# One GpSimd power in place of the Newton steps of the norms, two multiplications moved from GpSimd to VectorE, and the low part of the key copied over 128 partitions

## The chip, the cores and the metric

The kernel runs on one core of a Trainium2 chip. A core has TensorE (PE in the profile; its weight loads are listed apart as PEld), VectorE (DVE), ScalarE (ACT), GpSimd (POOL), and SyncE (SP), whose queue issues nearly all DMAs here. The metric is the device time of one execution in microseconds (us); less is better.

## The reference

The program is a two-layer encoder trunk on 512 tokens of width 1024. Each layer has a mixer (differential attention with 4 heads beside a bidirectional gated recurrence), a cross attention into 256 memory tokens and a squared-ReLU MLP, each behind an RMS norm. What the change touches:

```
y = x * rsqrt(mean(x*x) + 1e-6) * g                       # every norm
q, k = partial_rope(q), partial_rope(k)                   # t1*c - t2*s, t2*c + t1*s
s1, s2 = (q[..., 0] @ k1.T) / 8, (q[..., 1] @ k2.T) / 8   # two score maps of a head, 64 wide each
o = (softmax(s1) - lam * softmax(s2)) @ v
o = rms_norm(o, subln_g) * (1 - lam_init)                 # per head
u = x * i * sqrt(1 - a*a)                                 # i: a sigmoid gate, per channel and direction
```

All is computed in float32 accuracy: each operand of a product is split into a high and a low part, and a product is the sum of high x high, high x low and low x high.

## The kernel before, in words

**Layout.** Activations lie feature-major, 128 features by 512 tokens in a tile. A weight tile of 128x1024 is loaded (wraw), rounded by ScalarE to its high part (whi), and VectorE subtracts to get the low part (wlo). Tiles named b are 128x512 buffers (62 of them), s are columns of up to 8 numbers, mm and at are PSUM banks, pt holds transposed probabilities.

**Order of work.** Nothing is emitted where it is written. Every call is recorded with a key, which is the amount of TensorE work recorded before it (less a lead for loads and attention steps), and a list scheduler (Plan, from line 151; it emits at line 412) places the operations from a table of assumed costs (cost). Each engine then runs its instructions strictly in the order so found, so an operation that comes later than assumed holds up whatever stands behind it on its engine. All instructions therefore carry one line, 412; their tiles tell them apart.

**Layer.** First the value product and the norm of the input, then head 0's query and key. After that 16 attention steps (4 heads, 4 blocks of 128 queries), each with a piece of other work between its parts (fill): the query and key of the next heads (qk_head), the convolutions, gates and scans of the recurrence (lru_conv, lru_gates, lru_scan), the memory's keys and values. These stages lie at about 46 to 262 us in layer 0 and 785 to 1016 us in layer 1. Then come output projection, cross attention and MLP.

**Norms.** Norm.rstd (line 550) sums squares with TensorE against a column of ones, VectorE scales the sums (ms), rsqrt_small (line 495) computes ms to the power -1/2 by an integer guess and three Newton steps: ten VectorE instructions on at most 4 columns, each reading the one before. bcast (line 507) then spreads the columns with four TensorE transposes. There are 18 such roots: per layer three norms of x, one of the recurrence's output and four of the heads; one of the memory; and the final norm.

**Rotation and gates.** In qk_one (line 798) VectorE shuffles the product's partitions, multiplies it by the cosine table, GpSimd multiplies the shuffled copy by the sine table Sr, and VectorE adds: 16 times in all. In lru_gates (line 717) GpSimd multiplies the convolution's output by each input gate, also 16 times.

**Scores.** For one half j of a head, qk_head (line 814) stacks by DMA two 64-row parts of the query: m0 is high above low, m1 low above high. s0 and s1 hold the key's high part of half j twice, one copy over the other. So one product of 128 rows gives qh.kh + ql.kh. The rest, qh.kl, is a second product of 64 rows, taken from partitions 0 to 63 for j = 0 and 64 to 127 for j = 1:

```
PE.matmul(sc, mq, s_, start=True, stop=False)
PE.matmul(sc, m_[64 * j:64 * j + 64, qc * P:(qc + 1) * P],
          kl[64 * j:64 * j + 64, :], start=False, stop=True)
```

A step has two such pairs, a layer 32, the program 64.

Of the kernel before, what the change touches and what calls it, by code (L numbers as in the profile page):

```python
# [11 lines left out]
F32 = mybir.dt.float32  # L12
F32R = mybir.dt.float32r
I32 = mybir.dt.int32
AF = mybir.ActivationFunctionType
ALU = mybir.AluOpType
AX = mybir.AxisListType

P = 128
# [131 lines left out]
class Plan:  # L151
# [43 lines left out]
    def cost(self, eng, m, a, k):  # L195
        out = a[0] if a else k["out"]
        n = 1
        for d in out.shape[1:]:
            n *= d
        if eng == "pe":  # L200
            if m == "transpose":
                return 0.109
            f32 = a[1].root.dtype == F32
            if n < 64:
                return 0.224
            return n * 0.00176 if f32 else max(0.114, n * 0.000456)
        if m == "dma_start":
            return 0.06
        if eng == "act":
            t = 0.093 + n * 0.000833  # L210
            t += 0.093 * sum(isinstance(k.get(x), _View) for x in ("scale", "bias", "accum_out"))
            return t
        if eng == "dve":
            if m == "tensor_reduce":
                n = 512
            if m == "tensor_scalar_mul":
                return 0.066 + n * 0.0007
            ap = m == "scalar_tensor_tensor" and isinstance(a[2], _View)
            return 0.067 + n * 0.00105 + 0.06 * ap
        if eng == "pool":  # L220
            return 0.1 + n * (0.0022 if m != "memset" else 0.001)
        return 0.06
# [192 lines left out]
def trunk(tc, ctx, xT, memT, pos, W, par, outT):  # L415
# [10 lines left out]
    V, A, G, PE, SP = (plan.engine(e) for e in ("dve", "act", "pool", "pe", "sp"))  # L426

    def C(shape, dt, name):
        return plan.tile("c_" + name, shape, dt)

    def R():
        return plan.tile("b", [P, S], F32R)

    def T():
        return plan.tile("b", [P, S], F32)

    def SM(n):
        return plan.tile("s", [P, n], F32)

    def MM():  # L440
        return plan.tile("mm", [P, S], F32)

    def AT():
        return plan.tile("at", [P, S], F32)

    def b(v):
        return v.bitcast(F32)
# [24 lines left out]
    def weight(l, t):  # L472
        raw = pre.pop(t, None) if l == 0 else None
        first = raw is not None
        if raw is None:
            raw = raw_weight(l, t)
        hi = plan.tile("whi", [P, 1024], F32R)
        lo = plan.tile("wlo", [P, 1024], F32R)
        with plan.ahead(SPLIT_AHEAD):
            for cs in (slice(0, 512), slice(512, 1024)) if first else (slice(0, 1024),):  # L480
                split(hi[:, cs], lo[:, cs], raw[:, cs])
        return hi, lo

    def gemm_fm(l, t, xs, out, order=range(KD)):

        hi, lo = weight(l, t)
        for i, k in enumerate(order):
            xh, xl = xs[k]
            wh = hi[:, k * P:(k + 1) * P]
            with plan.group():  # L490
                PE.matmul(out, wh, xh, start=(i == 0), stop=False)
                PE.matmul(out, wh, xl, start=False, stop=False)
                PE.matmul(out, lo[:, k * P:(k + 1) * P], xh, start=False, stop=(i == KD - 1))

    def rsqrt_small(ms, n):

        y = SM(n)
        V.tensor_scalar(y.bitcast(I32), ms.bitcast(I32), -0.5, 1597463007.0,
                        op0=ALU.mult, op1=ALU.add)
        for _ in range(3):  # L500
            t = SM(n)
            V.tensor_tensor(t, y, y, op=ALU.mult)
            V.scalar_tensor_tensor(t, t, -0.5, ms, op0=ALU.mult, op1=ALU.mult)
            V.scalar_tensor_tensor(y, t, 1.5, y, op0=ALU.add, op1=ALU.mult)
        return y

    def bcast(col, ncol, out):
# [17 lines left out]
    def pc(l, name, i):  # L525
        o = l * NPL + PC[name] + i
        return prm[:, o:o + 1]
# [4 lines left out]
                    pattern=[[-1, P]], channel_multiplier=1)  # L532
    ones = C([P, P], F32, "ones")
    G.memset(ones, 1.0)

    class Norm:

# [179 lines left out]
    def lru_gates(l, pr, conv, neg, posi):  # L717

        gh, gl = weight(l, T_G + pr)
        gs = {}  # L720
        for c2 in range(2):
            c = 2 * pr + c2
            cc, ch, cl = conv[c]
            for d in range(2):
                for q in range(2):
                    pm = MM()
                    o = (4 * c2 + 2 * d + q) * P
                    with plan.group():
                        PE.matmul(pm, gh[:, o:o + P], ch, start=True, stop=False)
                        PE.matmul(pm, gh[:, o:o + P], cl, start=False, stop=False)  # L730
                        PE.matmul(pm, gl[:, o:o + P], ch, start=False, stop=True)
                    t = T()
                    A.activation(t, pm, AF.Sigmoid, bias=pc(l, "b_i" if q else "b_r", d * 4 + c))
                    if q:
                        G.tensor_tensor(t, cc, t, op=ALU.mult)
                    gs[c2, d, q] = t
        av = {}
        for c2 in range(2):
            for d in range(2):
                r = gs[c2, d, 0]  # L740
                col = l * 8 + d * 4 + 2 * pr + c2
                a, a2 = T(), T()
                A.activation(a, r, AF.Exp, scale=neg[:, col:col + 1])
                A.activation(r, r, AF.Tanh, scale=posi[:, col:col + 1])
                A.activation(a2, a, AF.Square)
                V.scalar_tensor_tensor(r, a2, 1.0, r, op0=ALU.add, op1=ALU.mult)
                av[c2, d] = a
        return gs, av
# [49 lines left out]
    def qk_one(l, t, xs, Cr, Sr, scale):  # L798
        pm = MM()
        gemm_fm(l, t, xs, pm)  # L800
        sh, q = T(), T()
        V.stream_shuffle(sh, pm, SHUF)
        V.tensor_tensor(q, pm, Cr, op=ALU.mult)
        G.tensor_tensor(sh, sh, Sr, op=ALU.mult)
        V.tensor_tensor(q, q, sh, op=ALU.add)
        hi, lo = R(), R()
        if scale is None:
            split(hi, lo, q)
        else:
            A.activation(hi, q, AF.Copy, scale=scale)  # L810
            V.scalar_tensor_tensor(lo, q, scale, b(hi), op0=ALU.mult, op1=ALU.subtract)
        return hi, lo

    def qk_head(l, h, xs, Cr, Sr):
        dm = SP.dma_start
        qh, ql = qk_one(l, T_FM + 2 * h, xs, Cr, Sr, 0.125)
        m0, m1 = R(), R()
        dm(out=b(m0[0:64, :]), in_=b(qh[0:64, :]))
        dm(out=b(m0[64:128, :]), in_=b(ql[0:64, :]))
        dm(out=b(m1[0:64, :]), in_=b(ql[64:128, :]))  # L820
        dm(out=b(m1[64:128, :]), in_=b(qh[64:128, :]))
        yield
        kh, kl = qk_one(l, T_FM + 2 * h + 1, xs, Cr, Sr, None)
        s0, s1 = R(), R()
        dm(out=b(s0[0:64, :]), in_=b(kh[0:64, :]))
        dm(out=b(s0[64:128, :]), in_=b(kh[0:64, :]))
        dm(out=b(s1[0:64, :]), in_=b(kh[64:128, :]))
        dm(out=b(s1[64:128, :]), in_=b(kh[64:128, :]))
        return m0, m1, s0, s1, kl

    def lam_col(l):
        pr = SM(2)
# [13 lines left out]
    class Head:  # L846
# [5 lines left out]
            self.pr, self.pt, self.o = {}, {}, None  # L852

        def scores(self, qc):
            m0, m1, s0, s1, kl = self.ops
            sums = self.sums
            es = []
            for j in range(2):
                m_, s_ = (m0, s0) if j == 0 else (m1, s1)
                sc = AT()  # L860
                mq = m_[:, qc * P:(qc + 1) * P]
                with plan.group():
                    PE.matmul(sc, mq, s_, start=True, stop=False)
                    PE.matmul(sc, m_[64 * j:64 * j + 64, qc * P:(qc + 1) * P],
                              kl[64 * j:64 * j + 64, :], start=False, stop=True)
                nmx = SM(1)
                V.tensor_reduce(nmx, sc, axis=AX.X, op=ALU.max, negate=True)
                e = T()
                A.activation(e, sc, AF.Exp, bias=nmx, accum_out=sums[:, 4 * j + qc:4 * j + qc + 1])
                es.append(e)  # L870
            rc = SM(1)
            V.reciprocal(rc, sums[:, 4 + qc:5 + qc])
            V.scalar_tensor_tensor(rc, rc, sums[:, qc:qc + 1], self.nlam, op0=ALU.mult, op1=ALU.mult)
            V.scalar_tensor_tensor(es[0], es[1], rc, es[0], op0=ALU.mult, op1=ALU.add)
            self.pr[qc] = es[0]
# [336 lines left out]
    for l in range(DEPTH):  # L1212
# [8 lines left out]
        Cr, Sr = rope_tables(sn, cs, rt)  # L1221
# [62 lines left out]
        for u in range(16):  # L1284
            h, qc = divmod(u, 4)
# [157 lines left out]
```

## Time and profile before

| | us |
|---|---|
| median of 3 runs | 1533.76 (1530.17 to 1539.23) |
| profiled execution, device time | 1536.88 |
| its span in the profile | 1535.1 |
| TensorE busy | 1476.1 (96%) |
| VectorE busy | 1183.5 (77%) |
| ScalarE busy | 727.1 (47%) |
| GpSimd busy | 54.1 (4%) |

The span is from the first to the last instruction of the profiled execution; 1.8 us of its device time lie outside. Matmuls are pipelined: one of 512 columns is shown with about 0.40 us though the next starts 0.23 us later, so a TensorE that is shown as wholly busy may still be losing time between starts. The clock that TensorE was granted is 1.00 (2.4 GHz) in most stretches and 0.5 (1.2 GHz) in some parts of the two attention stages.

### The profile page before, as it was taken

The page shows a single profiled execution, that of the slowest core. Times are in us where ns is not written, and L with a number is a line of the kernel's source. Part 1 is how long each engine was busy: PE and PEld are TensorE (multiplying, and loading weights), DVE is VectorE, ACT ScalarE, POOL GpSimd, SP SyncE. Part 2 cuts the span into 40 slices and gives each one's busy share as a digit, 9 for nine tenths or more (in the row PEclk, how much of TensorE's full clock was granted, in tenths as well). Part 3 has the DMA queues.
Part 4 walks back from the last instruction along what each step waited for, and adds up shares of the span by engine and source line. Part 5 has one row for each costly group of instructions (what it writes and reads, how often), then busy time and mean ns, then how long its engine had stood idle before and what let it go on. Part 6 is the DMA issues. An engine that isn't in the chain of part 4 may idle for free.

```text
span 1535.1 us, 20895 instructions
## 1 busy us (share of the span) xinstructions
PE 1476.1 (96%) x8038; PEld 1242.4 (81%) x8038; DVE 1183.5 (77%) x2107; ACT 727.1 (47%) x1099; POOL 54.1 (4%) x59
## 2 busy tenths in 40 slices
PE   8979999999999999999999799999999999999996
PEld 6757788888889889898977577888888898988985
DVE  7899886655589696979868876865656887969696
ACT  5587664444334343434535875553443433434243
POOL 0031000000000000000001310000000000000000
PEclk9989999999999999999999987999999999999998
DMA  5322342311222323222242213422112323232321
GB/s 194 97 82 78 129 138 82 110 69 56 96 96 83 110 84 122 98 97 97 87 134 81 85 57 110 144 101 96 55 69 82 110 84 107 86 110 83 116 88 58
DMA packets 45107, 148.24 MB, mean 97 GB/s; under 512 B 5584, under 2 KB 5712, under 8 KB 45008
## 3 DMA queue, kind: packets, MB, share of 16 engines
q1 hardware_dynamic: 44864, 146.65, 28.0%
q8 instruction: 63, 1.03, 0.3%
q14 instruction: 36, 0.29, 0.1%
q10 hardware_dynamic: 144, 0.26, 0.0%
HBM read 136.41 MB, written 2.10 MB: 90 GB/s over the span
## 4 chain that ended last, share of the span: by engine, by line
PE 85%; DVE 10%; issue 2%; DMA 1%; ACT 1%; SPq 0%; DVEq 0%; ACTq 0%
PE mm L412 65%; PE at L412 20%; DVE b L412 6%; DVE wlo L412 2%; DVE pt L412 1%; DVE s L412 1%; ACT b L412 1%; DMA b<-b 0%; DVE c_x L412 0%; DMA wraw<-in_W 0%; DMA c_x<-in_xT 0%; DMA wraw<-in_memT 0%; SPq L412 0%; ACT whi L412 0%; ACT Cr L412 0%
## 5 line engine op out<-in xcount | busy, mean ns | idle before, releaser
L412 PE MATMUL mm<-b,whi 128*128 128x512 f32 (+1 forms) x3648 | 991.3, 359 | 13.0 <-ACT b L412 6.2
L412 PEld LDWEIGHTS mm<-b,whi 128*128 128x128 f32 x3648 | 638.5, 190 | 126.3 <-ACT b L412 8.6
L412 PE MATMUL mm<-b,wlo 128*128 128x512 f32 (+1 forms) x1824 | 651.0, 357 | 8.0 <-DVE wlo L412 8.0
L412 ACT ACTIVATE whi<-wraw 128x1024 fp32r<-128x1024 f32 (+1 forms) x223 | 233.7, 1049 | 372.6 <-issue 168.3
L412 PEld LDWEIGHTS mm<-b,wlo 128*128 128x128 f32 x1824 | 345.8, 190 | 64.7 <-DVE wlo L412 10.0
L412 DVE TENSOR_TENSOR wlo<-wraw,whi 128x1024 fp32r<-128x1024 f32 (+1 forms) x223 | 277.1, 1243 | 37.2 <-ACT whi L412 36.9
L412 DVE TENSOR_TENSOR b<-b,b 128x512 fp32r<-128x512 f32 (+3 forms) x374 | 219.2, 602 | 15.6 <-ACT b L412 13.3
L412 ACT ACTIVATE b<-b 128x256 fp32r<-128x256 f32 (+2 forms) x224 | 130.3, 596 | 151.9 <-DVE b L412 151.3
L412 DVE TENSOR_TENSOR c_x<-c_x,mm 128x256 f32<-128x256 f32 (+1 forms) x160 | 73.8, 472 | 73.0 <-PE mm L412 71.6
L412 ACT ACTIVATE whi<-pt 128x1024 fp32r<-128x1024 f32 x64 | 67.9, 1061 | 101.6 <-PE mm L412 75.5
L412 PE MATMUL at<-b,whi 128*128 128x256 f32 x512 | 91.8, 278 | 0.0
L412 DVE TENSOR_TENSOR b<-mm,rb 128x512 f32<-128x512 f32 x72 | 49.5, 687 | 53.2 <-PE mm L412 52.5
L412 PE MATMUL at<-b,b 128*128 128x256 f32 (+1 forms) x320 | 83.9, 371 | 3.1 <-DVE b L412 2.2
L412 ACT ACTIVATE b<-at,s 128x512 f32<-128x512 f32 (+2 forms) x100 | 61.0, 614 | 41.9 <-DVE s L412 41.4
L412 DVE TENSOR_TENSOR wlo<-pt,whi 128x1024 fp32r<-128x1024 f32 x64 | 78.2, 1221 | 0.6 <-ACT whi L412 0.3
L412 DVE TENSOR_REDUCE s<-at 128x1 f32<-128x512 f32 (+1 forms) x80 | 54.4, 688 | 31.3 <-PE at L412 31.3
L412 PEld LDWEIGHTS at<-b,whi 128*128 128x128 f32 x512 | 77.6, 188 | 0.0
L412 PEld LDWEIGHTS at<-b,b 128*128 128x128 f32 x320 | 50.1, 195 | 30.9 <-issue 22.6
L412 PE MATMUL at<-b,wlo 128*128 128x256 f32 x256 | 71.1, 278 | 0.0
L412 PE MATMUL at<-pt,b 128*128 128x256 f32 (+1 forms) x288 | 53.1, 332 | 4.2 <-ACT pt L412 2.9
L412 PEld LDWEIGHTS at<-pt,b 128*128 128x128 f32 x288 | 45.3, 200 | 12.2 <-ACT pt L412 3.9
L412 DVE TENSOR_TENSOR c_x<-c_x,at 128x256 f32<-128x256 f32 x96 | 40.1, 419 | 18.1 <-PE at L412 17.7
(124 smaller groups left out, 1311.4 us busy)
## 6 DMA issues: line engine op xcount, KB each, us to landing
wraw<-in_W SPq DMA_DIRECT2D x249, 512.0 KB, 3.2
b<-b SPq DMA_DIRECT2D x64, 128.0 KB, 2.4
wraw<-in_memT SPq DMA_DIRECT2D x4, 512.0 KB, 3.9
out_T<-b SPq DMA_DIRECT2D x8, 256.0 KB, 2.6
c_x<-in_xT SPq DMA_DIRECT2D x7, 256.0 KB, 5.5
wraw<-in_W SPq DMA_DIRECT2D x6, 256.0 KB, 5.5
c_x<-in_xT ACTq DMA_DIRECT2D x1, 256.0 KB, 3.3
c_prm<-in_par SPq DMA_DIRECT2D x1, 89.0 KB, 3.2
```

The source lines that it names most:

```text
L412: getattr(self.engines[op.eng], m)(*a, **k)
```

## The change

rsqrt_small becomes one GpSimd instruction that raises ms to the power in a constant column (-0.5); the ten VectorE instructions go. The two kinds of 128x512 multiplications on GpSimd become VectorE instructions. qk_head gets two new tiles l0 and l1, each filled by two DMAs of 64x512 with the key's low part of half j, one copy over the other. The second score product then takes all 128 rows of m_ against l_: qh.kl + ql.kl, so the term low x low is added too. The planner's table gives GpSimd instructions of up to 4 columns a cost of 1.0 us; this also covers the small fills of xb.

```
 (in cost)
+        if eng == "pool" and n <= 4:
+            return 1.0
...
     def rsqrt_small(ms, n):
 
         y = SM(n)
-        V.tensor_scalar(y.bitcast(I32), ms.bitcast(I32), -0.5, 1597463007.0,
-                        op0=ALU.mult, op1=ALU.add)
-        for _ in range(3):
-            t = SM(n)
-            V.tensor_tensor(t, y, y, op=ALU.mult)
-            V.scalar_tensor_tensor(t, t, -0.5, ms, op0=ALU.mult, op1=ALU.mult)
-            V.scalar_tensor_tensor(y, t, 1.5, y, op0=ALU.add, op1=ALU.mult)
+        G.tensor_tensor(y, ms, mhalf[:, :n], op=ALU.pow)
         return y
...
+    mhalf = C([P, 4], F32, "mhalf")
+    G.memset(mhalf, -0.5)
...
                     if q:
-                        G.tensor_tensor(t, cc, t, op=ALU.mult)
+                        V.tensor_tensor(t, cc, t, op=ALU.mult)
...
-        G.tensor_tensor(sh, sh, Sr, op=ALU.mult)
+        V.tensor_tensor(sh, sh, Sr, op=ALU.mult)
...
         dm(out=b(s1[64:128, :]), in_=b(kh[64:128, :]))
-        return m0, m1, s0, s1, kl
+        l0, l1 = R(), R()
+        for j, t in enumerate((l0, l1)):
+            for i in range(2):
+                dm(out=b(t[64 * i:64 * i + 64, :]), in_=b(kl[64 * j:64 * j + 64, :]))
+        return m0, m1, s0, s1, l0, l1
...
-                m_, s_ = (m0, s0) if j == 0 else (m1, s1)
+                m_, s_, l_ = (m0, s0, l0) if j == 0 else (m1, s1, l1)
...
-                    PE.matmul(sc, m_[64 * j:64 * j + 64, qc * P:(qc + 1) * P],
-                              kl[64 * j:64 * j + 64, :], start=False, stop=True)
+                    PE.matmul(sc, mq, l_, start=False, stop=True)
```

The number of matmuls stays; VectorE gets 32 instructions and loses 180, SP gets 32 DMAs of 64x512. ScalarE's table loads, which follow from the order in which the planner puts its functions, go from 26 to 32. Lines move by two (412 becomes 414). Where the change moves instructions is shown at three places.

**VectorE, layer 1, the norm of head 0, before.** s_1630 is ms, s_1627 the reciprocal of the softmax sums, s_1631 the root; at_1629 holds the sums of squares.

```order
L412 TENSOR_SCALAR s_1630_8192<-s_1630_8192 128x4
L412 TENSOR_TENSOR b_1621_8194<-b_1621_8194,b_1620_8185 128x512
L412 SCALAR_TENSOR_TENSOR b_1577_8010<-b_1586_8105,b_1579_8016 128x512
L412 TENSOR_SCALAR s_1631_8263<-s_1630_8192 128x4
L412 TENSOR_REDUCE s_1663_8269<-at_1662_8189 128x1
L412 TENSOR_TENSOR b_1573_7988<-b_1573_7988,b_1577_8010 128x512
L412 TENSOR_TENSOR s_1632_8272<-s_1631_8263 128x4
L412 TENSOR_REDUCE s_1666_8274<-at_1665_8196 128x1
L412 SCALAR_TENSOR_TENSOR s_1632_8272<-s_1632_8272,s_1630_8192 128x4
L412 TENSOR_TENSOR pt_1680_8281<-at_1681_8200,pt_1679_8222 128x512
L412 SCALAR_TENSOR_TENSOR s_1631_8263<-s_1632_8272,s_1631_8263 128x4
L412 TENSOR_TENSOR b_1623_8292<-b_1621_8194,b_1622_8276 128x512
```

The same place now; s_1615 is ms, s_1616 the root that GpSimd writes.

```order
L414 TENSOR_TENSOR s_1615_8098<-at_1614_8087,s_1612_7877 128x4
L414 SCALAR_TENSOR_TENSOR s_1615_8098<-s_1615_8098,s_1612_7877 128x4
L414 TENSOR_SCALAR s_1615_8098<-s_1615_8098 128x4
L414 STREAM_SHUFFLE b_1603_8110<-mm_1599_8040 128x512
L414 SCALAR_TENSOR_TENSOR b_1560_8036<-b_1570_8101,b_1560_8036 128x512
L414 TENSOR_TENSOR s_1616_8108<-s_1616_8108,s_1612_7877 128x4
```

Before, the last of the root's instructions stands 19 rows behind the first and the product with the reciprocal one more, with eight instructions over 512 columns mixed in. Now two instructions over 512 columns stand between ms and the product that takes the root.

**ScalarE, layer 0, the gates of the second channel pair, before.** c_dneg and c_dpos mark the gates' Exp and Tanh, at,s the Exp of the softmax; an instruction from a b into the same b is here the square root.

```order
L412 ACT_TABLE_LOAD
L412 ACTIVATE b_259_1091<-b_244_1050,c_dneg_83_336 128x512
L412 ACTIVATE b_261_1110<-b_248_1068,c_dneg_83_336 128x512
L412 ACTIVATE b_232_1118,s_229_1119<-at_230_1088,s_231_1104 128x512
L412 ACTIVATE b_235_1128,s_229_1119<-at_233_1094,s_234_1112 128x512
L412 ACTIVATE b_269_1136,s_229_1119<-at_267_1098,s_268_1121 128x512
L412 ACTIVATE b_272_1148,s_229_1119<-at_270_1101,s_271_1126 128x512
```

The same place now.

```order
L414 ACTIVATE b_263_1126<-b_250_1054,c_dneg_81_338 128x512
L414 ACTIVATE b_250_1054<-b_250_1054,c_dpos_82_340 128x512
L414 ACTIVATE b_234_1149,s_231_1150<-at_232_1133,s_233_1139 128x512
L414 ACT_TABLE_LOAD
L414 ACTIVATE b_246_1042<-b_246_1042 128x512
L414 ACT_TABLE_LOAD
L414 ACTIVATE b_237_1162,s_231_1150<-at_235_1141,s_236_1152 128x512
L414 ACTIVATE b_271_1166,s_231_1150<-at_269_1136,s_270_1144 128x512
```

The four softmax exponentials stood together; now a single square root stands between the first and the second, with a table load on each side of it.

**SP, layer 0, head 0's copies, before.** b_102 and b_103 are the query's parts, b_112 the key's high part; in_W rows are weight loads.

```order
L412 DMA b_105_551<-b_103_538 64x512
L412 DMA b_105_551<-b_102_533 64x512
L412 DMA wraw_208_572<-in_W 128x1024
L412 DMA b_114_581<-b_112_574 64x512 x2
L412 DMA b_115_587<-b_112_574 64x512 x2
L412 DMA wraw_220_617<-in_W 128x1024
```

The same place now; b_110 is the key's high part and b_111 its low part.

```order
L414 DMA b_103_533<-b_100_520 64x512
L414 DMA wraw_208_562<-in_W 128x1024
L414 DMA b_112_574<-b_110_567 64x512 x2
L414 DMA b_113_577<-b_110_567 64x512 x2
L414 DMA b_114_583<-b_111_572 64x512 x2
L414 DMA b_115_590<-b_111_572 64x512 x2
L414 DMA wraw_220_610<-in_W 128x1024
```

Four copies of the low part stand between the high part's copies and the next weight load.

## Rows read from the trace of the kernel before

**Rows 1.** The page: span; busy us, share of the span, instructions by engine.

```profile
span 1535.1 us, 20895 instructions
...
PE 1476.1 (96%) x8038; PEld 1242.4 (81%) x8038; DVE 1183.5 (77%) x2107; ACT 727.1 (47%) x1099; POOL 54.1 (4%) x59
```

**Rows 2.** The page's chain that ended last, shares by engine.

```profile
PE 85%; DVE 10%; issue 2%; DMA 1%; ACT 1%; SPq 0%; DVEq 0%; ACTq 0%
```

**Rows 3.** Busy time by stretch; length, PE, PEld, DVE, ACT, POOL, clock, DMA share, GB/s.

```profile
46.00:94.00 48.00, 47.52 (x203) 35.49 (x202) 39.76 (x60) 34.13 (x56) 8.84 (x14) 1.00 0.26 85
94.00:156.00 62.00, 51.03 (x195) 36.76 (x193) 57.25 (x92) 47.41 (x76) 12.21 (x7) 0.86 0.29 87
156.00:262.00 106.00, 105.85 (x601) 87.34 (x602) 87.32 (x196) 60.86 (x106) 2.60 (x2) 0.98 0.37 124
...
785.00:865.00 80.00, 78.59 (x344) 58.66 (x343) 65.37 (x115) 50.33 (x83) 13.50 (x14) 1.00 0.32 99
865.00:935.00 70.00, 55.39 (x218) 40.97 (x218) 59.80 (x103) 50.90 (x83) 10.59 (x7) 0.86 0.32 99
935.00:1016.00 81.00, 81.00 (x465) 68.42 (x465) 61.23 (x136) 43.47 (x70) 0.00 (x0) 0.91 0.31 108
```

**Rows 4.** PE timeline, scores between weight products; start, us until the last end, instruction, count.

```profile
818.83 0.81 PE L412 MATMUL at<-b,b 128*128 128x512 f32 x2
819.57 0.73 PE L412 MATMUL mm<-b,whi 128*128 128x512 f32 x2
820.14 0.39 PE L412 MATMUL mm<-b,wlo 128*128 128x512 f32 x1
...
821.92 0.39 PE L412 MATMUL mm<-b,whi 128*128 128x512 f32 x1
```

**Rows 5.** Groups by form: the 64-row products in the whole span.

```profile
L412 PE MATMUL at<-b,b 64*128 64x512 f32 x64 | 34.3, 536 | 2.2 <-DVE b L412 2.2
```

**Rows 6.** The same form in the stretch 94 to 156 us.

```profile
L412 PE MATMUL at<-b,b 64*128 64x512 f32 x8 | 4.8, 606 | 2.2 <-DVE b L412 2.2
```

**Rows 7.** The same form in the stretch 865 to 935 us.

```profile
L412 PE MATMUL at<-b,b 64*128 64x512 f32 x8 | 5.1, 644 | 0.0
```

**Rows 8.** GpSimd's groups by form: the two kinds of multiplications that move.

```profile
L412 POOL TENSOR_TENSOR b<-b,b 128x512 f32<-128x512 f32 x16 | 26.6, 1678 | 50.5 <-ACT b L412 50.3
L412 POOL TENSOR_TENSOR b<-b,Sr 128x512 f32<-128x512 f32 x16 | 22.4, 1398 | 768.3 <-ACT Sr L412 647.5 <-DVE b L412 94.2 <-ACT whi L412 26.6
L412 POOL TENSOR_TENSOR b<-b,rb 128x512 f32<-128x512 f32 x2 | 2.5, 1267 | 610.0 <-ACT rb L412 610.0
```

**Rows 9.** DVE timeline in layer 0's gates.

```profile
104.08 1.26 DVE L412 TENSOR_TENSOR b<-b,b 128x512 f32<-128x512 f32 x2
105.26 1.22 DVE L412 TENSOR_TENSOR_SCAN b<-b,b 128x512 f32<-128x512 f32 x1
106.39 3.38 DVE L412 TENSOR_TENSOR b<-b,b 128x512 f32<-128x512 f32 x2
```

**Rows 10.** POOL timeline of the same moment.

```profile
104.02 5.21 POOL L412 TENSOR_TENSOR b<-b,b 128x512 f32<-128x512 f32 x2 [7.34 <-ACT b L412]
```

**Rows 11.** PE timeline at layer 1's first head norm; in brackets idle before.

```profile
873.53 0.40 PE L412 MATMUL mm<-b,wlo 128*128 128x512 f32 x1
883.77 1.08 PE L412 MATMUL at<-c_ident,s 128*128 128x128 f32 x4 [9.84 <-ACT b L412]
884.50 1.50 PE L412 MATMUL at<-b,b 128*128 128x512 f32 x2
885.93 1.11 PE L412 MATMUL at<-c_ident,b 128*128 128x128 f32 x4
```

**Rows 12.** DVE timeline of the same place: ms, and the root's first instruction.

```profile
874.60 1.22 DVE L412 TENSOR_SCALAR s<-s 128x4 f32<-128x4 f32 x1
...
877.47 0.14 DVE L412 TENSOR_SCALAR s<-s 128x4 int32<-128x4 int32 x1
```

**Rows 13.** Timeline of the final norm: ms, the root's first instruction, its transposes.

```profile
1522.53 0.16 DVE L412 TENSOR_SCALAR s<-at 128x4 f32<-128x4 f32 x1 [1.14 <-PE at L412]
1522.72 0.17 DVE L412 TENSOR_SCALAR s<-s 128x4 int32<-128x4 int32 x1
...
1524.72 1.11 PE L412 MATMUL at<-c_ident,s 128*128 128x128 f32 x4 [2.23 <-DVE s L412]
```

**Rows 14.** ScalarE's table loads, by form.

```profile
L412 ACT ACT_TABLE_LOAD x26 | 33.4, 1283 | 1.6 <-PEq L1435 1.2
```

**Rows 15.** SP's issues of head 0's key copies in layer 1.

```profile
800.09 2.39 SPq L412 DMA_DIRECT2D b<-b  x4
```

More of the change, by code (lines that the diff above doesn't have):

```diff
@@ L854, in scores @@
         def scores(self, qc):
-            m0, m1, s0, s1, kl = self.ops
+            m0, m1, s0, s1, l0, l1 = self.ops
             sums = self.sums
```

## The prediction

> **What bounds the kernel now.** I read the page's shares first, then the chain of waits, then busy time by stretch, then the timelines of the places where a stretch departs from the rest. The chain ends last through TensorE for 85% of the span and through VectorE for 10% [rows 2]. The change touches the two attention stages nearly alone, and these fall into two kinds of stretches [rows 3]. From 46 to 94, 156 to 262, 785 to 865 and 935 to 1016 us TensorE is busy to at least 98%: what counts there is what a product costs. From 94 to 156 and 865 to 935 us it is busy for 51.03 of 62 and 55.39 of 70 us at a granted clock of 0.86, that is, part of it at the lower of its two levels, and VectorE is the busiest engine (57.25 and 59.80 us). There TensorE waits for VectorE, and what counts is how long VectorE's queue is and what stands in its order.
>
> **The score products (removes).** Where scores stand between weight products, the pair starts at 818.83 and the next low weight product at 820.14, with two high ones between: four products in 1.31 us. From 820.14 to 821.92 stand a low product, a second such pair with its two high products, and another low product: 1.78 us, less 1.31 leaves 0.47 for two plain products, 0.235 each [rows 4]. Four plain products would take 0.94, so a pair costs 0.37 us more than its columns ask for, before, between or after its 64-row member. After the change all four are products of 128 rows, and I take the 0.37 as gone wholly (bounds: nothing gone, or all). There are 64 pairs [rows 5]; 8 start in each of the two VectorE-bound stretches [rows 6, 7], where a faster product only waits longer. The other 48 give 48 x 0.37 = -17.8 us. What is late next there is VectorE, which still has a sixth to a quarter of these stretches idle [rows 3].
>
> **The multiplications on GpSimd (moved).** The 32 cost GpSimd 26.6 + 22.4 us [rows 8]. On VectorE two such multiplications take 1.18 us from the start of the first to the start of what follows, 0.59 each: 32 x 0.59 = 18.9 us more for VectorE. But the same kind of pair takes 3.38 us beside GpSimd's multiplications at 104 to 109 us, 2.2 us more for two GpSimd instructions, so up to 1.06 us each is held up today [rows 9, 10]. That is a bound of 1.06 x 32 = 34 us given back against 18.9 us added; the other bound is that nothing is given back. VectorE instructions that read PSUM beside GpSimd are not held up, so I take about 0.6 given back for each and a net of nothing, between -7 and +8 us for the 14 of the two VectorE-bound stretches (7 GpSimd instructions in each [rows 3]).
>
> By the Trainium skill (SBUF — State Buffer, section "SBUF: two separate sides") GpSimd and VectorE share one port pair as an exclusive lock: whoever starts first keeps it for its whole instruction, the other waits. The rows just read agree (one VectorE pair, 2.2 us longer). The rule speaks against the new power too, since it reads SBUF: each would hold VectorE for its own length, and would itself wait behind VectorE. Counted so, with 1.3 us each for the three powers in the VectorE-bound stretches, the sum below would be 4 us worse.
>
> **The roots (removed and added).** A root alone takes from 1522.72 to the transposes at 1524.72: 2.0 us of VectorE's time and of latency [rows 13]. The power on GpSimd is shown by no row: it lies between nothing and 3.5 us, the length of the longer of GpSimd's two multiplications at 104 us if the other takes the mean of 1.68 [rows 8, 10]. I take 1.3 us, the shortest 512-column instruction there [rows 8], and 0.2 us for the hand-over. At the end that gives 2.0 - 1.5 = -0.5 us. At the norms between stages TensorE has products to do meanwhile; the new order leaves nine plain products there (2.1 us) where twelve stood, so nothing is gained and nothing lost while the power keeps below about 1.3 us. In the stretch 94 to 156 us one root stands in VectorE's own chain: -1.9 us.
>
> One root is worth more. In layer 1 TensorE stops at 873.9 and starts the transposes of head 0's root at 883.77, 9.84 us later [rows 11]. The profile names ScalarE, but these transposes read the root, and its instructions run from 877.47 on, spread among eight long ones of VectorE (the order shows that). Ms itself took 1.22 us instead of 0.16 beside a GpSimd multiplication [rows 12, 13]. Now two long instructions stand between ms and the product with the root. From ms's undisturbed end (874.60 + 0.16) I count 1.5 for the power, 0.2 for the product, 0.1 to TensorE: transposes at 876.6, -7.2 us. After the stop TensorE ran at half clock: a score pair with start at 884.50 took 1.43 us, where the one at 818.83 took 0.74, so 0.7 each for at least four pairs; -3 us with the shorter stop (bounds 0 and -6).
>
> **Table loads (added).** Six more at 1.283 us = 7.7 us on ScalarE [rows 14], all between gates and scores; two enclose a single square root and delay three exponentials for which VectorE and then TensorE wait. ScalarE is busy for 47.41 of 62 and 50.90 of 70 us there, so some hide in its idle time. Bounds 0 and +7.7; I take half, +3.9 us.
>
> **Copies of the low part (added).** Four more issues a head: 2.39 us for four today [rows 15], 19 us in all on SP. For heads 1 to 3 they lie under the step before. Head 0's scores wait for the last of them in both layers: +2.4 us less 1.2 for the rotation's shorter way through VectorE (1.40 - 0.59, and a hand-over saved), so +1.2 twice, +2.4 us (bounds 0 and +4.8). Behind them in SP's order stands one weight load.
>
> **Sum.** -17.8 - 0 - 0.5 - 1.9 - 7.2 - 3 + 3.9 + 2.4 = -24.1 us on an execution of 1536.88 us (span 1535.1 [rows 1], 1.8 outside): 1512.8. The median of the runs shown is 3.1 us below that execution, so the sum on it is 1509.7. I forecast **1510 us**.
>
> **Rivals.**
> 1. *VectorE and ScalarE take the gain.* The planner has counted all score products at the plain rate all along, so TensorE's lag of 0.37 us a pair has been slack for the others. Without it TensorE arrives on time and waits for reductions and exponentials: a third of the 17.8 stays (-6), the table loads cost their whole 7.7, the 9.84 us stop moves to another place of the new order, -5 stays. About -6 - 5 - 2.4 + 7.7 + 2.4 = -3: 1531 us. For it: VectorE above 90% of the VectorE-bound stretches; against it: it loses 180 small instructions there and elsewhere. 12%.
> 2. *More than the sum.* With the held-up VectorE instructions gone, both VectorE-bound stretches shorten by more: 11 and 15 us of TensorE's idle time lie in them [rows 3], and half of it with its half clock is about 15 us beyond the sum, and the loads hide: 1492 us. For it: every long gap of TensorE's lies there. 22%.
> 3. *The power is slow.* One mechanism, at the transposes behind each root. Nine products hide 2.1 us, of which sums and ms use up to 1; what the power takes over 1.3 us TensorE waits at up to 18 roots, also through the VectorE product that waits for the root in its queue at the eight head norms. 24.1 / 18 = 1.3, so from 2.6 us on the kernel is slower than before; at 3.5 us it is 1510 + 18 x 2.2 = 1550 us. For it: no row shows a power on GpSimd. Against it: its 512 columns of a multiplication take 1.3 us, and this has four. 11%.
> 4. *The 64-row product isn't the cause.* The 0.37 us come from the change between scores and weight products: then 17.8 falls away, -6, 1527 us. Against it: 64-row products take 536 ns on the mean [rows 5], plain ones 0.39. 7%.
>
> The forecast itself has 48%. What a measurement of this kernel tells from no change is about 0.5%, 7.7 us: from 1526.1 to 1541.4. Faster by more: nearly all of the forecast, rival 2, a third of rival 4 and a quarter of rival 1, 0.74 in all. Within: most of what is left of both, and the part of rival 3 below its point, 0.15. Slower: the rest of rival 3 and a sixth of rival 1, 0.11. The forecast's own range is 1500 to 1524; the range for 8 in 10 goes from 1490 (rival 2) to 1536 (rivals 1 and 4, a power of up to 2.6 us).
>
> **What would show it.** No 64-row form in the groups, score pairs at 0.47 us from start to start, TensorE's gaps before weight products behind scores gone. VectorE at about 1183.5 - 30 us busy, with no small instruction at 1.2 us. The new form on GpSimd 18 times; its mean decides rival 3. The two VectorE-bound stretches shorter, with no stop of 9.84 us before transposes of a root. Table loads 32. It would be wrong if score pairs kept their 0.37 us, if TensorE waited for the root at several norms, or if stops before scores grew beside table loads.

## The result, and the profile after

The changed kernel takes 1509.97 us (median, 1508.43 to 1510.51) against 1532.16 (1530.17 to 1539.23): ratio 0.9845, 95% interval 0.9812 to 0.9879. Measured again beside the first experiments it took 1508.45 (ratio 0.9826, 0.9801 to 0.9851). The forecast was 1510. The total came out right. The experiments show that the score products carry it, as predicted, and that most of what was booked to one root belongs to the order of instructions.

The page of the changed kernel answers to [rows 1]: TensorE is busy 29 us less, VectorE 24 us less though it took over 32 long instructions.

```profile
span 1506.6 us, 20763 instructions
...
PE 1446.8 (96%) x8038; PEld 1239.1 (82%) x8038; DVE 1159.3 (77%) x1959; ACT 731.7 (49%) x1105; POOL 26.5 (2%) x46
```

Busy time by stretch, columns as in [rows 3]:

```profile
46.00:94.00 48.00, 46.37 (x211) 36.94 (x209) 42.01 (x70) 36.12 (x60) 0.53 (x8) 1.00 0.32 94
94.00:156.00 62.00, 49.02 (x198) 38.52 (x199) 51.90 (x85) 46.86 (x72) 1.01 (x1) 0.81 0.39 105
156.00:262.00 106.00, 101.99 (x605) 89.01 (x604) 84.40 (x151) 66.71 (x115) 5.69 (x5) 0.98 0.39 127
...
865.00:935.00 70.00, 64.82 (x356) 54.25 (x355) 67.15 (x112) 54.29 (x90) 2.32 (x2) 0.98 0.43 128
```

Layer 1's gates (last row) now keep TensorE busy for 64.82 instead of 55.39 us at a clock of 0.98 instead of 0.86. Layer 0's gates did not gain like that: 49.02 against 51.03, and the stretch behind them, full before, now has 4 us of idle TensorE.

Groups by form: the score products are all of one shape, the power is there 17 + 1 times.

```profile
L414 PE MATMUL at<-b,b 128*128 128x512 f32 x128 | 42.7, 429 | 5.8 <-DMA b<-b 3.7 <-ACT b L414 1.7 <-PE at L414 0.2
L414 POOL TENSOR_TENSOR s<-s,c_mhalf 128x4 f32<-128x4 f32 x17 | 20.6, 1210 | 1395.7 <-DVE s L414 1395.7
L414 POOL TENSOR_TENSOR s<-s,c_mhalf 128x2 f32<-128x2 f32 x1 | 0.7, 697 | 0.3 <-DVE s L414 0.3
L414 ACT ACT_TABLE_LOAD x32 | 41.1, 1283 | 1.7 <-PEq L1436 1.2
```

Timelines at three places: a score pair among weight products, head 0's norm in layer 1 (answers to [rows 11, 12]), and the final norm (answers to [rows 13]).

```profile
822.58 0.63 PE L414 MATMUL at<-b,b 128*128 128x512 f32 x2
823.05 0.62 PE L414 MATMUL mm<-b,whi 128*128 128x512 f32 x2
823.51 0.39 PE L414 MATMUL mm<-b,wlo 128*128 128x512 f32 x1
...
862.32 0.17 DVE L414 TENSOR_SCALAR s<-s 128x4 f32<-128x4 f32 x1
862.66 1.01 POOL L414 TENSOR_TENSOR s<-s,c_mhalf 128x4 f32<-128x4 f32 x1 [49.97 <-DVE s L414]
863.97 0.15 DVE L414 TENSOR_TENSOR s<-s,s 128x4 f32<-128x4 f32 x1
865.59 0.60 PE L414 MATMUL at<-c_ident,s 128*128 128x128 f32 x4
...
1494.88 0.16 DVE L414 TENSOR_SCALAR s<-at 128x4 f32<-128x4 f32 x1 [1.15 <-PE at L414]
1495.19 1.01 POOL L414 TENSOR_TENSOR s<-s,c_mhalf 128x4 f32<-128x4 f32 x1 [342.70 <-DVE s L414]
1496.25 1.11 PE L414 MATMUL at<-c_ident,s 128*128 128x128 f32 x4 [1.41 <-POOL s L414]
```

The pair and two high products take 0.93 us to the low product (823.51 - 822.58), where they took 1.31 [rows 4]. The transposes at 865.59 wait for nothing: the 9.84 us stop is gone. The final norm takes 1.37 us from ms to the transposes instead of 2.19.

To see where time is won, I counted TensorE's products at their plain rate (the work) and took the start of the product at the same work in both traces. The difference, after less before:

```
work   before   after   difference (us)
  80     92.9    90.0    -2.8   scores of layer 0
 100    133.1   132.9    -0.1   gates of layer 0
 260    304.8   301.0    -3.8   end of layer 0's attention
 800    860.6   858.9    -1.7   layer 1, before the 9.84 us stop
 820    900.9   884.2   -16.6   behind the stop and its half clock
 860    953.4   928.2   -25.2
1400   1505.7  1478.0   -27.7   end
```

Layer 0 brings 3.8 us, layer 1 some 24, and nearly all of that between work 800 and 860. Of the 8.6 us from 820 to 860, most is a wait of 2.9 us and 17 us at half clock (0.50) behind it in the execution of before that was profiled:

```profile
933.00:950.00 17.00, 16.42 (x65) 14.38 (x66) 9.10 (x34) 6.85 (x11) 0.00 (x0) 0.50 0.17 60
...
933.32 0.58 PE L412 MATMUL at<-pt,b 128*128 128x256 f32 x1 [2.90 <-ACT pt L412]
```

Such parts differ from run to run: eleven further runs of before lasted 1530.3 to 1538.8 us, at a mean clock of 0.983 in the shortest and 0.975 to 0.977 in the four longest. The profiled one is a long one, 4.7 us above its median. So the medians decide below, and differences between two traces are used for the place only.

### The profile page after: what moved, and what is told of

It reads as the page before. It is cut to its first block, busy times and chain, and to the rows that moved or that the text cites. A ratio compares the mean times of both kernels' runs of the same rounds, so it can differ in the third digit from the quotient of the medians.

```text
span 1506.6 us, 20763 instructions
## 1 busy us (share of the span) xinstructions
PE 1446.8 (96%) x8038; PEld 1239.1 (82%) x8038; DVE 1159.3 (77%) x1959; ACT 731.7 (49%) x1105; POOL 26.5 (2%) x46
## 4 chain that ended last, share of the span: by engine, by line
PE 80%; DVE 11%; ACT 4%; issue 2%; DMA 1%; SPq 1%; POOL 0%; DVEq 0%; ACTq 0%; POOLq 0%
PE mm L414 63%; PE at L414 18%; DVE b L414 6%; DVE wlo L414 3%; ACT b L414 3%; DVE pt L414 1%; ACT L414 1%; SPq L414 1%; DMA b<-b 1%; DVE s L414 1%; ACT whi L414 0%; POOL s L414 0%; DVE c_x L414 0%; DMA wraw<-in_memT 0%; DMA c_x<-in_xT 0%
## 5 line engine op out<-in xcount | busy, mean ns | idle before, releaser
L414 PE MATMUL mm<-b,wlo 128*128 128x512 f32 (+1 forms) x1824 | 650.1, 356 | 10.2 <-DVE wlo L414 10.2
L414 DVE TENSOR_TENSOR wlo<-wraw,whi 128x1024 fp32r<-128x1024 f32 (+1 forms) x223 | 268.9, 1206 | 40.9 <-ACT whi L414 40.4
L414 DVE TENSOR_TENSOR b<-b,b 128x512 fp32r<-128x512 f32 (+2 forms) x390 | 224.7, 593 | 16.0 <-ACT b L414 14.4
L414 PE MATMUL at<-b,b 128*128 128x256 f32 (+1 forms) x320 | 67.3, 341 | 5.8 <-DMA b<-b 3.7
L414 DVE TENSOR_TENSOR c_x<-c_x,at 128x256 f32<-128x256 f32 x96 | 40.0, 417 | 18.4 <-PE at L414 17.8
```

The source lines that it names most:

```text
L414: getattr(self.engines[op.eng], m)(*a, **k)
```

## The experiments

Each of the three parts was tried three ways: taken back in the changed kernel with every instruction in its place (e1 to e3); done alone in the kernel before, with the order planned anew (e4 to e6); and done alone in the kernel before with every instruction in its place (e9, e10, e12). Medians in us, as differences from the changed kernel measured beside them (1508.45) for the first column and from the kernel before, measured beside each group of runs (1535.05, 1534.03 and 1531.81), for the others:

| part | taken back in the new order | alone, planned anew | alone, old order |
|---|---|---|---|
| second product over 128 rows | +15.4 | -8.3 (with copies) | -20.5 (no copies) |
| multiplications on VectorE | +6.1 | -18.2 | -0.2 |
| roots by the power | +17.1 | -5.9 | -0.5 |
| all three | | -26.6 (first time -22.2) | -23.5 (no copies) |

Each ratio's interval is 0.4 to 0.5% wide, so a difference is good to some 3 us, one between two kernels of the experiments to some 5. The first two columns don't add up to the whole (38.6 and 32.4 us against 26.6): what a part is worth depends on the order that it stands in. In the old order the parts add up to it within noise (21.2 against 23.5).

**The changed kernel again (a1_after).** 

> The changed kernel once more, beside the others of this call, as what they are measured against: 1510 us, within 3 us of its first time.

Measured 1508.45 us, as above.

**The second product over 64 rows, new order (e1_rows64).**

```
-                    PE.matmul(sc, mq, l_, start=False, stop=True)
+                    PE.matmul(sc, m_[64 * j:64 * j + 64, qc * P:(qc + 1) * P],
+                              l_[64 * j:64 * j + 64, :], start=False, stop=True)
```

> The changed kernel with every instruction in its place, but the second product of each score pair over the 64 rows that hold numbers, as before the change; the copies of the low part stay. Theory (a pair costs 0.37 us more around its 64-row member, and 48 of the 64 pairs stand where TensorE sets the time): 16 to 24 us slower than the changed kernel, 1526 to 1534 us, and a pair with its two weight products takes 1.31 us again instead of 0.94. A weaker form of it (the cost is there, but in the gate stretches something else ends last): 4 to 12 us slower, 1514 to 1522 us. Rival (the cost came from the change between scores and weight products): within 3 us of the changed kernel.

Measured 1523.89 us (ratio 0.9928, 0.9905 to 0.9951), 15.4 more, just short of the theory's 16 to 24. On TensorE's timeline a pair with its two high products now takes 1.34 us again (65.40 - 64.06), 0.41 more than in the changed kernel:

```profile
64.06 0.83 PE L417 MATMUL at<-b,b 128*128 128x512 f32 x2
64.82 0.74 PE L417 MATMUL mm<-b,whi 128*128 128x512 f32 x2
65.40 0.40 PE L417 MATMUL mm<-b,wlo 128*128 128x512 f32 x1
```

15.4 / 0.41 is 38 of the 64 pairs; the prediction had 48 at 0.37. The rival (the change between scores and weight products) falls: that change is there in both kernels.

**The multiplications on GpSimd, new order (e2_mulpool).** The 32 instructions keep their places and are issued on GpSimd (`G` for `V` at emission).

> The changed kernel with every instruction in its place in the order, but the 32 multiplications issued on GpSimd again. Theory (what VectorE saves, some 19 us, it loses again in being held up beside GpSimd): the multiplications are worth nothing either way, between 7 us faster and 8 us slower than the changed kernel, with VectorE's instructions beside GpSimd some 20 us longer in sum. Rival (VectorE's held-up instructions were what filled the two gate stretches): 8 to 15 us slower, nearly all of it in layer 1's gate stretch.

Measured 1514.53 us (0.9868, 0.9844 to 0.9892), 6.1 more, inside the theory's range, and VectorE's instructions beside GpSimd's are 20.9 us longer in sum, as the theory had it. The traces put nearly all of it into layer 0 (6.9 of 7.9), not into layer 1's gates, so the rival's place is wrong.

**The root by ten VectorE instructions, new order (e3_newton).** At the place of each power the integer guess and three steps are issued on VectorE.

> The changed kernel with every instruction in its place in the order, but each root worked out by VectorE's ten small instructions where the power now stands. Theory: 2.0 us instead of 1.4 at 18 roots, of which some lie under products: 2 to 8 us slower than the changed kernel. Rival (the power on GpSimd with its hand-over costs as much as the ten instructions, and the gain of the roots lies in the order alone): within 2 us. A second rival (the power is the slower one): 2 to 6 us faster.

Measured 1525.54 us (0.9939, 0.9919 to 0.9960), 17.1 more: above all expectations. VectorE's timeline at head 0's norm in layer 1 shows how a root costs time there:

```profile
871.25 0.17 DVE L417 TENSOR_SCALAR s<-s 128x4 int32<-128x4 int32 x1
...
873.03 0.16 DVE L422 SCALAR_TENSOR_TENSOR s<-c_scr,s 128x4 f32<-128x4 f32 x1
...
874.34 0.16 DVE L424 TENSOR_TENSOR s<-s,s 128x4 f32<-128x4 f32 x1
```

From 871.25 to 873.1 VectorE's strict queue does nothing but the root, each step reading the one before; the shuffle and the rotation behind it start that much later. In the old order the ten were spread among long instructions and cost their busy time only. This one norm accounts for some 2.5 of the 15 us between the traces. The largest step, some 5 us, is at a norm of layer 0, where TensorE waits longer for the transposes and then runs at half clock to 202 us instead of 195; first with the ten instructions, then in the changed kernel:

```profile
198.00 1.10 PE L424 MATMUL at<-c_ident,s 128*128 128x128 f32 x4 [3.35 <-ACT b L424]
...
192.01 1.10 PE L414 MATMUL at<-c_ident,s 128*128 128x128 f32 x4 [2.24 <-ACT b L414]
```

So part of the 17.1 us is clock and not VectorE's time.

**One part alone, planned anew (e4_score_only, e5_norm_only, e6_mul_only).** The three diffs are the pieces of the change shown above, each by itself.

> The kernel before with the score part of the change alone (both products over 128 rows, the low part copied), its order planned anew: 30 table loads. Theory (the parts stand for themselves; 48 pairs at 0.37 us, less 2.4 us for head 0's copies and half of four table loads): 1532 - 17.8 + 2.4 + 2.6 = 1519 us, 1513 to 1525. Rival (a faster product only waits for VectorE as long as the roots and multiplications are as before, so that the parts pay only together): 1526 us or more.

> The kernel before with the power on GpSimd alone, its order planned anew: 26 table loads as before. Theory (the sum's terms for the roots: end -0.5, one root in VectorE's own chain -1.9, the 9.84 us stop -7.2 and its half clock -3): 1532 - 12.6 = 1519 us, 1514 to 1525. Rival (that stop goes through another part or the order alone, and the roots are worth only the few tenths of their length): 1526 to 1532 us. A second rival, from the run with VectorE's ten instructions in the changed kernel's order (17 us slower): the power is worth all of that by itself, 1512 to 1516 us.

> The kernel before with the 32 multiplications on VectorE alone, its order planned anew: 34 table loads, eight more. Theory (net of nothing, and half of the eight loads): 1532 + 5 = 1537 us, 1530 to 1542. Rival (in the changed kernel's order they were worth 6 us, and are so here): 1522 to 1528 us.

Measured: scores 1525.74 us (0.9936, 0.9919 to 0.9953), between theory and rival; roots 1528.10 (0.9950, 0.9932 to 0.9967), the first rival; multiplications 1515.82 (0.9876, 0.9858 to 0.9894), better than any expectation, with eight more table loads. TensorE's timeline at head 0's norm in layer 1, roots alone:

```profile
877.58 1.12 PE L414 MATMUL at<-c_ident,s 128*128 128x128 f32 x4 [5.47 <-DVE pt L414]
...
883.83 2.96 PE L414 MATMUL at<-b,b 128*128 128x512 f32 x4 [2.94 <-ACT b L414]
```

And multiplications alone, where the root still has its ten instructions:

```profile
870.96 0.60 PE L412 MATMUL at<-c_ident,s 128*128 128x128 f32 x4
...
875.50 0.73 PE L412 MATMUL mm<-b,whi 128*128 128x512 f32 x2 [1.55 <-ACT b L412]
```

With the power alone the stop became two waits of 5.47 and 2.94 us; with the scores alone one of 8.5 us stays; with the multiplications alone it went, though that order has another wait ahead of the place, of 3.30 us for copies:

```profile
841.30 4.38 PE L412 MATMUL at<-b,b 128*128 128x512 f32 x6 [3.30 <-DMA b<-b]
```

That the root's ten instructions make the stop has fallen. Two causes were left: VectorE being held up beside GpSimd, or the order that the planner finds.

**The same parts in the old order (e9_before_mul, e10_before_pow, e12_whole_only).** In e9 the 32 multiplications are issued on VectorE at their old places; in e10 the power stands at the place of the root's first instruction; in e12 the second product takes the whole of mq and the whole of kl:

```
-                    PE.matmul(sc, m_[64 * j:64 * j + 64, qc * P:(qc + 1) * P],
-                              kl[64 * j:64 * j + 64, :], start=False, stop=True)
+                    PE.matmul(sc, mq, kl, start=False, stop=True)
```

> The kernel before with every instruction in its place, but the 32 multiplications issued on VectorE. Theory (the 9.84 us stop of layer 1 comes of VectorE's queue, held up beside GpSimd's multiplications, and not of the root that ends last in it): the stop shrinks to under 4 us though the root keeps its ten instructions, and the kernel is 10 to 20 us faster than before. Rival (it is the root's, and moving the multiplications is worth a net of nothing): the stop stays at 7 us or more, within 6 us of before. Second rival (the stop goes by the new order alone, as in the replanned kernel with this part): the same.

> The kernel before with every other instruction in its place, but each root as one power on GpSimd at the place of the root's first instruction. Theory of the prediction (the stop of 9.84 us is the root's ten instructions spread among long ones): the stop falls by about 7 us, the kernel is 10 to 13 us faster than before. Rival (the stop is VectorE's queue beside GpSimd): the stop moves to another wait of 5 us or more, or the power itself waits behind GpSimd's multiplications, and the kernel is 0 to 6 us faster.

> The kernel before with every instruction in its place, but the second product of a score over 128 rows, reading the key's low part whole without any copy (so the query's low part meets the other half's low part, a term as small as the one left out before). Theory (48 pairs at 0.37 us, no copies, no new table loads): 12 to 18 us faster than before. Rival (what the pairs give, the stops of the gate stretches take back as long as VectorE is held up): 4 to 9 us faster, as the replanned kernel with this part alone was.

Measured: e9 1531.59 us (0.9992, 0.9974 to 1.0011), e10 1531.27 (1.0000, 0.9982 to 1.0018), e12 1511.33 (0.9872, 0.9851 to 0.9893): e9 and e10 within noise of no change, e12 a little above its theory. In e9 the stop stays at 9.53 us, TensorE's timeline:

```profile
880.06 1.09 PE L413 MATMUL at<-c_ident,s 128*128 128x128 f32 x4 [9.53 <-ACT b L413]
```

I had expected the opposite. VectorE was held up much less there: taking from each of its instructions that overlaps a GpSimd multiplication or power the median of its form, the excess is 17.8 us over 68 instructions in the kernel before (39 of them work on SBUF alone and have all of it; the 29 that read PSUM have 0.03 us) and 0.0 us in e9. But VectorE also got 32 x 0.59 us of work, and its busy time stayed (1183.5 and 1184.6). The held-up instructions are not the stop's cause. In e10 the row of the root's user tells it:

```profile
870.32 5.03 POOL L416 TENSOR_TENSOR b<-b,b 128x512 f32<-128x512 f32 x2 [5.31 <-ACT b L416]
875.45 1.38 POOL L414 TENSOR_TENSOR s<-s,c_mhalf 128x4 f32<-128x4 f32 x1
...
877.03 0.66 DVE L416 TENSOR_REDUCE s<-at 128x1 f32<-128x512 f32 x1
...
882.31 0.16 DVE L416 TENSOR_TENSOR s<-s,s 128x4 f32<-128x4 f32 x1
...
882.61 1.09 PE L416 MATMUL at<-c_ident,s 128*128 128x128 f32 x4 [9.13 <-DVE s L416]
```

The power is done at 876.83; the product with it stands behind ten other VectorE instructions and starts at 882.31, so TensorE still stops for 9.13 us. A shorter root is worth next to nothing here as long as its user keeps its place in the queue. (An order that moves this user alone was not tried.)

**The copies (e7_nocopy).** The changed kernel without its 32 copies; the second product reads kl whole, everything else in its place.

> The changed kernel with every other instruction in its place, without the 32 copies of the low part: the second product of a score reads the key's low part whole, so that the query's low part meets the other half's low part, a term as small as the one left out before. Theory (head 0's scores wait for the last copy in both layers): 2 to 5 us faster than the changed kernel, 1504 to 1507 us, at two places, 55 and 803 us. Rival (the copies also push back the weight load behind them on SP at 155 us): 5 to 9 us faster. Null: within 1.5 us.

Measured 1501.42 us (0.9783, 0.9764 to 0.9801): 7.0 less than the changed kernel, good to some 5 us, so the time alone decides neither for the theory nor for the rival; the place does, for the rival. The changed kernel: SP's issues in layer 0, the load on the chain that ended last, and TensorE's wait for head 0's copies in layer 1:

```profile
146.40 4.95 SPq L414 DMA_DIRECT2D b<-b  x8
151.44 1.22 SPq L414 DMA_DIRECT2D wraw<-in_memT  x2
...
151.44 4.31 DMA wraw<-in_memT
...
803.88 1.39 PE L414 MATMUL at<-b,b 128*128 128x512 f32 x5 [0.64 <-DMA b<-b]
```

SP's issues without the copies:

```profile
144.59 2.39 SPq L419 DMA_DIRECT2D b<-b  x4
147.51 3.33 SPq L419 DMA_DIRECT2D wraw<-in_memT  x2
```

Eight copies hold SP for 4.95 us where four hold it for 2.39, and they start 1.8 us later, since the changed kernel is behind already at that point; so the load of the memory is issued 3.9 us later, and it is on the chain there. By the traces 6.1 of the 8.2 us between them lie in layer 0, only some 1 at each head 0. This is what layer 0 lacks in the table by work: without the copies it wins some 9 us, and with the score part alone in the old order (e12) some 11, against 3.8.

**All three in the old order (e13_three_old_order).** e9, e10 and e12 together, 26 table loads, no copies.

> The kernel before with every other instruction in its place and all three edits at once: multiplications on VectorE, the power at the place of the root's first instruction, the second score product over 128 rows without copies; 26 table loads as before. Theory (the parts' gains are the operations' own, the new order gives little): 1495 to 1506 us, near the changed kernel without copies (1501 us). Rival (the new order is what makes the gain of the changed kernel): 1510 us or more.

Measured 1508.36 us (0.9851, 0.9833 to 0.9869): between the two. Beside e12 (1511.33) the other two parts bring 3 us, no more than noise, though VectorE is busy for 1159.6 instead of 1181.9 us; and the stop is still there, 7.47 us; the power is held up beside VectorE, but done at 863.44, and the product with it stands at 867.85:

```profile
860.46 2.98 POOL L414 TENSOR_TENSOR s<-s,c_mhalf 128x4 f32<-128x4 f32 x1 [56.55 <-DVE s L417]
...
867.85 0.16 DVE L417 TENSOR_TENSOR s<-s,s 128x4 f32<-128x4 f32 x1
...
868.15 1.09 PE L417 MATMUL at<-c_ident,s 128*128 128x128 f32 x4 [7.47 <-DVE s L417]
```

So with VectorE neither held up nor given the roots the stop remains: 4.4 us of it are the place of the root's user in the order, and most of the rest is the power, held up to 2.98 us. The changed kernel without copies (e7, 1501.42 us) is 7 us better than this one with six table loads more; it beats both kernels of the case, and is the version to keep. What the six loads cost by themselves was not tried.

## Why the prediction was right, step by step

- **Score products, -17.8: right.** In the old order the part alone gave -20.5 us, in the new order it takes 15.4 back. The price of a pair is 0.41 us instead of 0.37, and the two gains are those of 50 and 38 pairs, where the prediction had 48. By the Trainium skill (TensorEngine Tiling (Array Packing), section "Key Properties") a change of the tiling mode drains TensorE; the rows agree in that pairs of one shape lose nothing, but no run here shows that a drain is what the 0.41 us are.
- **Multiplications, net of nothing: right as an operation, wrong as an edit.** In the old order -0.2 us: 18.9 us added, 17.8 given back. Planned anew the same edit gives -18.2. The step that failed is that the term priced VectorE's busy time alone, and not what the planner makes of the edit. By the rule of the Trainium skill on the shared ports (SBUF — State Buffer, section "SBUF: two separate sides") a VectorE instruction with two SBUF inputs and a GpSimd instruction that reads SBUF hold each other up. The trace agrees (17.8 us in sum, none of it in instructions that read PSUM); the end did not move with it. But not every instruction beside GpSimd is held up: the pair of 1.26 us that the prediction took as undisturbed lay beside the same GpSimd instructions [rows 9, 10]. And beside the powers of the changed kernel no VectorE instruction was longer (0.03 us in sum over 24), so the 4 us that the prediction worked out for them by that rule did not come.
- **Roots: the end about right (0.8 us against 0.5), "one root is worth more" wrong in its cause.** The 9.84 us stop was put down to the root's ten instructions, and the power and its product counted as the cure (-7.2, and -3 for the half clock). The stop is the order's: the power alone leaves 9.13 us of it in the old order and 8.4 in two pieces when planned anew, and the multiplications alone, planned anew, remove it with the old root. That it would go in this change was read rightly from the new order. Between work 800 and 820 of the traces 14.9 us went, against 10.2 counted, but that figure holds the gain of the 8 score pairs there too [rows 7]: with these alone, and the stop still there (e12), some 3 us go. The new order was planned with the short root and needs it: there the ten instructions cost 17.1 us, clock included.
- **Copies, +2.4: too small, 7.0 measured.** "For heads 1 to 3 they lie under the step before" is the sentence that failed: in layer 0 the memory's load stands behind eight copies on SP. At each head 0 the traces show some 1 us, near the 1.2 counted.
- **Table loads, +3.9: open.** There are 32 as said; no run separates them.
- **Rivals.** A slow power (rival 3): 1.01 us where VectorE is quiet, 2.98 at the worst, and 1.21 on the mean, below its point of 2.6. More than the sum through VectorE set free (rival 2): from e12 to e13 VectorE has 22 us less to do, and the end moves by 3. The taken gain (rival 1): 6 us go back in layer 0, but through the copies, which is not its mechanism. The change between scores and weight products (rival 4): e1 refutes it.

So the total was right in part by luck. By the medians the score products alone (e12) gave 20.5 us instead of 17.8. From e12 to the changed kernel without copies (e7), that is, for the roots, the multiplications and the new order with its table loads, it is 9.9 us; the prediction had 8.7 there (0.5 + 1.9 + 7.2 + 3 - 3.9), booked to the roots. The old order makes 3 us of the same edits. The copies took 7.0 back instead of 2.4. Each of these is good to some 5 us only, so which error made up for which is not shown.

## What to carry to other kernels

In a kernel whose engines follow a planned order, price an edit twice: once with every instruction in its place, which gives what the operation is worth, and once planned anew, which gives what the order makes of it; here the same edit was worth 0 and 18 us. A stop that ends with some instruction need not be that instruction's cost: look where its user stands in the queue. Small DMAs cost their place in the issuing queue: at 0.62 us an issue here, ask what stands behind them.

## What was unexpected of the hardware

- A power of 128x4 on GpSimd takes 1.01 us in 11 of the 17 cases in the changed kernel, and more, up to 2.98 (in the last experiment), only beside VectorE's long instructions. The one of two columns took 0.70 there, and 1.14 to 1.20 beside such instructions in the old order.
- A 64-row float32 product between 128-row ones costs 0.41 us more for the pair, although it feeds the same number of columns; a product over the full 128 rows, with numbers that weigh nothing in half of them, is the cheaper one.
- VectorE's instructions that read PSUM are not held up beside GpSimd's multiplications (0.03 us in sum over 29), those that work on SBUF alone are (17.8 us over 39).
- 22 us of VectorE's work could be taken away (e12 to e13) for 3 us at the end, no more than noise, as long as the order stayed.
